# A hybrid decoder step on one core: a normalisation moved to ScalarE for a third token group, GpSimd and SyncE loads held by a VectorE instruction, and block-product operands paired otherwise

## The chip, the core and the metric

The kernel runs on one core of a Trainium2 chip. The core has five engines, each with its own instruction queue that it works in order: TensorE (PE in the profile; matrix products and transposes), VectorE (DVE), ScalarE (ACT), GpSimd (POOL) and SyncE (SP). Engines wait for each other through semaphores. All but PE and VectorE also start DMA transfers here, and a transfer's start stands in the queue of the engine that starts it. The metric is device time in microseconds (us); lower is better.

## The reference

One layer: a modulated RMSNorm, one input projection, two groups of heads (a gated linear recurrence, RG-LRU, and gated linear attention, GLA), one output projection, a gate, the residual and a last RMSNorm. There are 2048 prompt tokens of 1024 features and 8 single tokens of decoding ("samples") with their own state.

```python
hn = _rmsnorm(x, g_norm) * (1.0 + scale[:, None]) + shift[:, None]
z = hn @ w_in
xa, za, q, k, v, glr, zg = jnp.split(z, SPLITS, axis=-1)
...
a = jnp.exp(log_a)
u = mult * (gx * xc).astype(f32)
_, h = lax.associative_scan(_lin_comb, (a, u), axis=1)
y_lru = h.astype(x.dtype) * jax.nn.silu(za)
...
o, S_new = _gla_chunked(qh, kh, vh, log_alpha, S0.astype(f32))
o = o * lax.rsqrt(jnp.mean(o * o, axis=-1, keepdims=True) + EPS) * g_gla_norm.astype(f32)
y_gla = o.reshape(Bn, T, D_GLA).astype(x.dtype) * jax.nn.silu(zg)
mix = jnp.concatenate([y_lru, y_gla], axis=-1) @ w_out
x = x + gate[:, None] * mix
```

The columns of `w_in` are called XA, ZA, Q, K, V, GLR and ZG in the kernel. `xc` is a convolution over four tokens of `xa`, `h` the recurrence; v has 4 heads of 256 columns, and GLR's 16 columns drive the decay of the attention.

## The kernel before

**Numbers.** Every large product is made of three: a float32 operand is split into a rounded half (`hh`, "hi") and the remainder (`hl`, "lo"), and hi·hi, hi·lo and lo·hi are summed in PSUM, PE's accumulator memory. `hh` and `hl` hold the normalised input of 1024 tokens, features on the partitions, as (128, 8, 1024+64). So a line of products in the profile has two sisters (L661, L662, L663; L346, L347, L348).

**Halves.** The prompt is worked in two halves of 1024 tokens. In each half the four attention heads come in the order `HEADS` = 3, 0, 1, 2, and between them the tiles of the recurrence (128 channels each). Work that an engine is to do "somewhat later" is put on a list (`after(units, fn)`) and taken from it when `tick` has counted that many units; a second list, `drips`, is emptied one entry at a time between products.

**Between the halves** `hh` and `hl` are filled anew: `modulate(xt, g, kts)` takes one of four groups of 256 tokens (g = 0 to 3), two feature tiles (k2, k2+1) at a time. PE transposes four 128×128 blocks into a PSUM buffer of the tag "tp", of which there are two (L197). ScalarE scales and shifts the first feature tile out of it (L199); the second goes to ScalarE (L201) for g < 2, else to VectorE (L203). GpSimd rounds into `hh` (L204), and VectorE subtracts for `hl` (L205). Ahead of a group, VectorE multiplies its rows with reciprocal roots (L181). At the same time the first half's last recurrence tile runs (L1304 to L1338), and ZG of the first head (`gates_ahead`; L661–663, L1115, L1116, the store L1633 from ScalarE's queue).

**Block products.** For the second half, ZG of three heads and XA and ZA of two recurrence tiles are made by a scheme that needs seven block products in place of eight (`seven`, `product`, PE line L1545; five such sevens, so 35 operands of weights). The sums of blocks that it needs are made in `sums` (L1479 to L1488). The sums overwrite a quarter of the normalised input (`a21()`, the first four feature tiles of tokens 512 to 1023, 1 MB in `hh` and 1 MB in `hl`); a copy is kept in DRAM (`a21d`). An operand of weights is 512 KB, loaded by SP (L1527), and two operands share one buffer of the tag "w", of which there are three (`operand`): 1 and 2, 3 and 4, and so on; the 35th has a buffer to itself. A buffer is free when both its operands are used.

**A head of the second half** (`gla_head(1, h, ahead)`): `value_weights` has SP load the split weights of V in two parts of 1 MB (L293, tag "w"). For the first head, GpSimd then reads `a21` back (L1164–1166). `values` makes eight tiles of 128 tokens (L346–348; n = 272 columns for the first head, which has GLR with it, 256 for the others); each is copied out by ScalarE (L944) and VectorE (L945), and for the first head the 16 GLR columns are transposed and copied by VectorE (L876–878). Tiles 4 to 7 are the tokens that `a21` belongs to. At tile 2, `raw_values` starts two loads of the unsplit weights on GpSimd (L333, 512 KB each, tag "wr", of which there are two), which `sample_values` uses for the 8 samples (PE L900, VectorE L904) after the eight tiles; the first 32 matmuls of L900 use the first load, the other 32 the second. Then the decay, Q and K follow in segments, the chunks of the attention (L1029 and others), and the next recurrence tile, whose XA weights are loaded by `ahead` (SP, L293).

GpSimd's queue in these heads also has `zs<-zgd` (L1196, gates read back), and the preparation of output weights: `r` loads from `w_out` (L817), VectorE's products and sums (L838), and stores `wd<-r`, `wd<-t` (L852).

**Final products.** Before the end of the second half, `early` holds the first steps of the final products: for two pairs, `first` adds two blocks of `mixd` that SP loaded to `wr` (L1949), subtracts a third (L1950) and splits (L1680, L1683).

**Order.** A scheduler decides each engine's order from the traced program; the order of tracing counts, and so do waits. `behind(q)` (L683) adds an edge to the scheduler's order alone: what is traced inside is not issued ahead of the last instruction traced on q. It makes no semaphore wait.

Of the kernel before, what the change touches and what calls it, by code (L numbers as in the profile page):

```python
# [8 lines left out]
F32 = mybir.dt.float32  # L9
# [3 lines left out]
OP = mybir.AluOpType  # L13
# [41 lines left out]
def hybrid_kernel(ctx, tc, i, o):  # L55
# [131 lines left out]
    def modulate(xt, g, kts):  # L187

        c = slice(g * 256, (g + 1) * 256)
        for k2 in range(kts[0], kts[1], 2):  # L190
            pt = tps().rearrange("p (k t) -> p k t", k=2)
            cg = slice(g % 2 * 256, g % 2 * 256 + 256)
            f = (fs4[(1, 2, 0)[k2 // 4 if g < 2 else 2]][:, k2 % 4:k2 % 4 + 2, cg] if g < 2 or k2 >= 4
                 else ra[k2 // 2][:, :, cg])
            for kt in range(2):
                for j in range(2):
                    PE.transpose(pt[:, kt, j * P:(j + 1) * P],  # L197
                                 xt[j][:, (k2 + kt) * P:(k2 + kt + 1) * P], ident)
            S.activation(f[:, 0], pt[:, 0], AF.Identity, scale=Gm[:, k2, 8:9], bias=Sh[:, k2, 8:9])  # L199
            if g < 2:  # L200
                S.activation(f[:, 1], pt[:, 1], AF.Identity, scale=Gm[:, k2 + 1, 8:9], bias=Sh[:, k2 + 1, 8:9])  # L201
            else:
                V.tensor_scalar(f[:, 1], pt[:, 1], Gm[:, k2 + 1, 8:9], Sh[:, k2 + 1, 8:9], op0=OP.mult, op1=OP.add)  # L203
            G.tensor_scalar(hh[:, k2:k2 + 2, c], f, 1.0, 0.0, op0=OP.mult, op1=OP.add)  # L204
            V.tensor_tensor(hl[:, k2:k2 + 2, c], f, hh[:, k2:k2 + 2, c].bitcast(F32), op=OP.subtract)  # L205
# [118 lines left out]
    def value_weights(h):  # L324
        n = DV + (RANK if h == HEADS[0] else 0)
        return [weights(V0 + h * DV, n, k0, 4) for k0 in (0, 4)]
# [356 lines left out]
        return tc.issue_after(next(x for x in reversed(list(nc.cur_bb.bb.instructions)) if x.engine == q.engine))  # L683


    pend = []
    clock = [0, 0]

# [229 lines left out]
            e[2]()  # L918
        return [[gp.tile([P, 4, DV], F32R, tag=tag, name=tag, bufs=2) for _ in range(2)] for tag in ("vh", "vl")]

    def values(half, h, w):
        first = h == HEADS[0]
        n = DV + (RANK if first else 0)
        vh, vl = new_values()
        turns = []
        for tt in range(8):
            if tt == 2 and half == 1:
                raw = raw_values(h, n)
            if tt == 4:
                while drips:  # L930
                    drip()
            if half == 0 or tt < 6:
                ps = acc()
                value_mm(ps[:, :n], slice(tt * P, (tt + 1) * P), w, n, (0, KT))
            elif tt == 6:
                both = [acc(), acc()]
                for k in (0, 4):
                    for m in range(2):
                        value_mm(both[m][:, :n], slice((6 + m) * P, (7 + m) * P), w, n, (k, k + 4))
                ps = both[0]  # L940
            else:
                ps = both[1]
            hi, lo = vh[tt // 4][:, tt % 4], vl[tt // 4][:, tt % 4]
            S.copy(hi, ps[:, :DV])  # L944
            V.tensor_tensor(lo, ps[:, :DV], hi.bitcast(F32), op=OP.subtract)  # L945
            if len(turns) == 3 or tt == 7 and turns:
                turns.pop(0)()
            if first:
                turns.append(low_rank(ps[:, DV:n], slice(0, P), tt * P))
            tick(0.5)  # L950
        if half == 1:
            turns.append(sample_values(h, raw, n))
        for f in turns:
            after(1, f, True)
        return vh, vl
# [201 lines left out]
    def gla_head(half, h, wv=None, ahead=None):  # L1157
        ns = len(SEGS[half])
        if wv:
            wk, wq = wkq0  # L1160
            v, prep0, rest = first_head()
        else:
            w = value_weights(h)
            if half and h == HEADS[0]:  # L1164
                for u, x in enumerate(a21()):
                    G.dma_start(x.bitcast(F32), a21d[u])
            v = values(half, h, w)
            wk = weights(K0 + h * DK, DK)
            wq = weights(Q0 + h * DK, DK)
        prep, zs, os_, state = {}, {}, [None], []  # L1170

        def chunks(s, c):

            nch = min(SEGS[half][s][1], TH - SEGS[half][s][0]) // P
            if c == 0:
                prep[s, "run"] = gla_start(half, h, s, prep[s])
                after(PACE[half][0], lambda: chunks(s, 1), True, True)
                return
            if c == nch and half:
                gate_load(s)  # L1180
            gla_chunk(half, h, s, c - 1, prep[s], prep[s, "run"], v)
            if c < nch:
                after(PACE[half][1], lambda: chunks(s, c + 1), True, True)
                return
            gla_norm(nch, prep[s, "run"])
            after(PACE[half][2] if half else 1 if s + 1 < ns else 2, lambda: finish(s), True)
            if s + 1 < ns:
                after(0, lambda: chunks(s + 1, 0), True, True)
            elif half == 1:
                G.dma_start(o[4][0, 0, h], St[h])  # L1190

        def gate_load(s):
            c0, n = SEGS[half][s]
            for dt in range(2):
                z = new_zs()
                G.dma_start(z[:, :n], zgd[2 * h + dt][:, c0:c0 + n])  # L1196
                zs[s, dt] = z[:, :n]

        def finish(s):
            if (s, 1) not in zs or (s == 2 and os_[0] is None):  # L1200
                after(0.5, lambda: finish(s), True)
                return
            gla_out(half, h, s, prep[s, "run"][1], os_[0] if s == 2 else None, [zs[s, 0], zs[s, 1]])

        def sample(smp, b0):
            sample_state(h, smp, b0, state, lambda: os_.__setitem__(0, state[1]))

        pk = None
        if not wv:
            if h == HEADS[0]:  # L1210

                pk = project(wk, *SEGS[half][0])
            dec = gla_decay(half, h, 0)
        for s in range(ns):
            if wv and s == 0:
                prep[s] = prep0
                pk = project(wk, 512, 512)
                rest()
            else:
                prep[s] = gla_qk(half, h, s, wq, wk, dec, pk)  # L1220
                pk = None
                if s == 0 and ahead:
                    with behind(V):
                        ahead()
            if s + 1 < ns:
                dec = gla_decay(half, h, s + 1)
            if s == 0:
                after(2 if h == HEADS[0] else 1, lambda: chunks(0, 0), True, True)
            tick()
        if half == 1:  # L1230
            after(1, lambda: sample(prep[2][3], 0), True)
            after(3, lambda: sample(prep[2][3], 4), True)
        if wv:
            modulate_samples(st, xsr)
            hn_sample()
            with tc.issue_after(last[V.engine]), tc.issue_after(last[S.engine]):
                constants()
            open_lp()
        if half == 1:
            return  # L1240
        wz = [weights(ZG + (2 * h + dt) * P, P) for dt in range(2)]
        for s in range(ns):
            for dt in range(2):
                zs[s, dt] = gate_silu(wz[dt], s, 2 * h + dt)
                tick()
# [266 lines left out]
        for n, u in ((0, 0), (1, 0), (0, 1), (1, 1), (2, 0), (2, 1), (3, 0), (3, 1), (4, 0), (4, 1)):  # L1512
            drips.append(lambda n=n, u=u: step(n, u))

    operands, zq, zturn = [], [], [0]

    def operand(src, shifted):

        if operands:
            c = 568 if shifted else 576  # L1520
            w = operands.pop()
        else:
            c = 56 if shifted else 0
            w = wp.tile([P, 2, 1088], F32R, tag="w", name="w", bufs=3)
            operands.append(w)
        w = w[:, :, c:c + 512]
        SP.dma_start(w.bitcast(F32), src)  # L1527
        return w.rearrange("p u (k n) -> p u k n", k=4)
# [413 lines left out]
    for x in pairs[:2]:  # L1942
        x.new(A11)
        r = wp.tile([P, 1088], F32, tag="wr", name="wr")[:, :D].rearrange("p (q k t) -> p q k t", q=2, k=4)
        SP.dma_start(r, mixd[2 * x.p + 1, :, CTS[0]:CTS[0] + 8].rearrange("p (q k) t -> p q k t", q=2))
        SP.dma_start(x.lo(A11), x.rows(0, 0))

        def first(x=x, r=r):
            V.tensor_tensor(r[:, 0], r[:, 0], r[:, 1], op=OP.add)  # L1949
            V.tensor_tensor(r[:, 0], r[:, 0], x.lo(A11), op=OP.subtract)  # L1950
            x.s[S2] = r[:, 0]
            x.split(A11)

        early += [first, lambda x=x: x.split(S2)]
# [288 lines left out]
```

## Time and profile before

| | us |
|---|---|
| three runs | 1466.02, 1466.95, 1469.85 |
| median | 1466.95 |
| the profiled execution, its own time | 1465.58 |
| its span, first to last instruction | 1463.8 |
| PE busy in the span | 1427.3 (98%) |
| VectorE busy | 1053.7 (72%) |
| ScalarE busy | 688.0 (47%) |
| GpSimd busy | 221.3 (15%) |

The mean granted clock of TensorE over the span is 0.994 of full speed. Rows of the timeline read: start, duration, engine, line, operation, output<-inputs, shapes, how many instructions (x); in brackets the idle time of the engine before it and what ended it (`<-DVE ra L203`: the wait ended when VectorE's line 203 had written `ra`). Rows of stretches read: from:to and length, then busy us and number of instructions for PE, PE's weight loads, VectorE, ScalarE and GpSimd, then the granted clock, the DMA engines' busy share and GB/s. In the list of waits the three figures are the total, the number and the longest.

### The profile page before, as it was taken

Reading aid. Unit: us, or ns where it says so; the run is one execution under the profiler, and the core shown is the slowest. Engines: PE = TensorE matmul, PEld = TensorE weight load, DVE = VectorE, ACT = ScalarE, POOL = GpSimd, SP = SyncE. Lnnn points to the kernel's source line nnn. Section 1 sums busy time; section 2 is a strip of 40 time slices with the busy share of each in tenths; the row PEclk is TensorE's granted clock in tenths of the full one; section 3 lists DMA queues with packets and bytes.
Section 4 is the critical chain, followed back from the end, with each engine's and each line's share of the span. In section 5 each row is a group of like instructions: output and inputs, shape, how many; then the busy total and the mean of one; then the engine's idle time right before and its main releaser. Section 6 shows DMA issues by size and latency. Waiting matters only on the chain. (4 is left out here: it accounts for less than half of the span.)

```text
span 1463.8 us, 23573 instructions
## 1 busy us (share of the span) xinstructions
PE 1427.3 (98%) x8741; PEld 1254.7 (86%) x8741; DVE 1053.7 (72%) x2481; ACT 688.0 (47%) x1247; POOL 221.3 (15%) x366
## 2 busy tenths in 40 slices
PE   7999999999999998999899999999999999999998
PEld 6888989899898987878799999999899887778886
DVE  5757657776666778845358688586788986688886
ACT  4644544652445457524354454535558622144342
POOL 0200111112121122100212332323200000000000
PEclk9999999999999999999999999999999999999999
DMA  9755876765666455567736665666453767694453
GB/s 332 259 184 173 268 250 212 253 218 180 201 200 218 131 185 204 191 221 242 278 122 205 221 207 168 209 209 227 163 196 110 273 209 271 238 360 124 141 174 115
DMA packets 161240, 305.33 MB, mean 209 GB/s; under 512 B 12962, under 2 KB 91458, under 8 KB 158685
## 3 DMA queue, kind: packets, MB, share of 16 engines
q1 hardware_dynamic: 104917, 214.24, 42.8%
q0 software_dynamic: 23296, 72.54, 14.6%
q10 hardware_dynamic: 32912, 17.04, 3.8%
q8 instruction: 69, 1.13, 0.3%
q14 instruction: 46, 0.38, 0.1%
HBM read 188.51 MB, written 115.33 MB: 208 GB/s over the span
## 5 line engine op out<-in xcount | busy, mean ns | idle before, releaser
L661 PE MATMUL acc<-hh,w 128*128 128x512 f32 (+3 forms) x1112 | 387.1, 348 | 0.3 <-ACT tg L1304 0.2
L662 PE MATMUL acc<-hl,w 128*128 128x512 f32 (+3 forms) x1112 | 376.3, 338 | 0.0
L663 PE MATMUL acc<-hh,w 128*128 128x512 f32 (+3 forms) x1112 | 375.8, 338 | 0.0
L661 PEld LDWEIGHTS acc<-hh,w 128*128 128x128 f32 x1112 | 210.3, 189 | 17.8 <-ACT tx L1304 0.5
L662 PEld LDWEIGHTS acc<-hl,w 128*128 128x128 f32 x1112 | 210.3, 189 | 17.5 <-issue 1.2
L663 PEld LDWEIGHTS acc<-hh,w 128*128 128x128 f32 x1112 | 210.0, 189 | 16.4
L1830 PE MATMUL acc<-w,a 128*128 128x512 f32 (+1 forms) x792 | 184.9, 387 | 0.0
L1830 PEld LDWEIGHTS acc<-w,a 128*128 128x128 f32 x792 | 146.8, 188 | 33.2 <-issue 3.4
L346 PE MATMUL acc<-w,hh 128*128 128x256 f32 (+1 forms) x508 | 145.3, 286 | 3.7 <-DMA w<-parts 3.7
L348 PE MATMUL acc<-w,hl 128*128 128x256 f32 (+1 forms) x508 | 143.7, 283 | 0.2 <-DVE hl L228 0.2
L347 PE MATMUL acc<-w,hh 128*128 128x256 f32 (+1 forms) x508 | 143.7, 283 | 0.0
L1830 PE MATMUL tp<-w,a 128*128 128x512 f32 x564 | 136.3, 391 | 0.3 <-DVE w L1683 0.3
L1830 PEld LDWEIGHTS tp<-w,a 128*128 128x128 f32 x564 | 105.2, 188 | 27.4 <-issue 5.1
L346 PEld LDWEIGHTS acc<-w,hh 128*128 128x128 f32 x508 | 96.5, 190 | 5.2 <-DMA w<-parts 3.9
L348 PEld LDWEIGHTS acc<-w,hl 128*128 128x128 f32 x508 | 96.8, 191 | 0.4 <-DVE hl L228 0.4
L347 PEld LDWEIGHTS acc<-w,hh 128*128 128x128 f32 x508 | 96.2, 189 | 0.2
L1115 ACT ACTIVATE zs<-acc 128x512 f32<-128x512 f32 (+3 forms) x70 | 34.3, 491 | 110.2 <-PE acc L663 107.7
L1264 DVE SCALAR_TENSOR_TENSOR cv<-xa,vecT,cv 128x512 f32<-128x512 f32 (+2 forms) x120 | 76.2, 638 | 6.8 <-ACT cv L1262 6.3
L1680 ACT CAST a<-s 128x512 fp32r<-128x512 f32 x61 | 36.5, 620 | 94.5 <-issue 34.0
L1116 DVE SCALAR_TENSOR_TENSOR zs<-zs,acc 128x512 f32<-128x512 f32 (+3 forms) x70 | 38.5, 550 | 48.6 <-ACT zs L1115 48.6
L944 ACT CAST vh<-acc 128x256 fp32r<-128x256 f32 x56 | 20.6, 370 | 97.6 <-PE acc L348 84.1
L945 DVE TENSOR_TENSOR vl<-acc,vh 128x256 fp32r<-128x256 f32 x56 | 23.3, 421 | 55.7 <-ACT vh L944 55.5
(404 smaller groups left out, 2749.4 us busy)
## 6 DMA issues: line engine op xcount, KB each, us to landing
parts<-w SPq DMA_DIRECT2D x37, 1024.0 KB
w<-parts SPq DMA_DIRECT2D x28, 1024.0 KB
wr<-in_w_in_dram SPq DMA_DIRECT2D x38, 512.0 KB
a<-mixd SPq DMA_DIRECT2D x63, 256.0 KB
w<-wd SPq DMA_DIRECT2D x12, 1024.0 KB
w<-twd SPq DMA_DIRECT2D x20, 512.0 KB
mixd<-zs ACTq DMA_DIRECT2D x34, 256.0 KB
wada<-in_w_ada_dram SPq DMA_DIRECT2D x16, 512.0 KB
```

The source lines that it names most:

```text
L346: PE.matmul(ps, hh[:, kt, c], hi[:, kt % 4], start=kt == 0, stop=False)
L347: PE.matmul(ps, hh[:, kt, c], lo[:, kt % 4], start=False, stop=False)
L348: PE.matmul(ps, hl[:, kt, c], hi[:, kt % 4], start=False, stop=kt == KT - 1)
L661: PE.matmul(ps[:, :n], hi[:, kt], a, start=kt == 0, stop=False)
L662: PE.matmul(ps[:, :n], hi[:, kt], b, start=False, stop=False)
L663: PE.matmul(ps[:, :n], lo[:, kt], a, start=False, stop=kt == KT - 1)
L945: V.tensor_tensor(lo, ps[:, :DV], hi.bitcast(F32), op=OP.subtract)
L1115: S.activation(z, ps, AF.Tanh, scale=0.5)
L1116: V.scalar_tensor_tensor(z, z, 1.0, ps, op0=OP.add, op1=OP.mult)
L1264: V.scalar_tensor_tensor(cv[:, cq], xa[:, cq.start + k:cq.stop + k], cw[k], cv[:, cq], op0=OP.mult, op1=OP.add)
L1680: S.copy(t[:, 0, k], (low(t) if src is None else src)[:, k])
L1830: PE.matmul(ps, t[:, u, k], w[:, v, k, c], start=(q < 3 or ps is own) and (k, u, v) == (0, 0, 0), stop=(k, u) == (3, 1), skip_group_check= ...
```

## The change

It has six parts.

1. `modulate`: the second feature tile goes to ScalarE for g < 3 instead of g < 2. For g = 2 four instructions of L203 become instructions of L201.
2. A new helper, `held(q)`: every SP or GpSimd instruction traced inside waits, by a semaphore, for the last instruction traced on engine q.
3. `values`: the two reads of `a21` (first head of the second half) are started at tile 1 instead of before tile 0, and held by VectorE. `raw_values` is started at tile 3 instead of tile 2, held by VectorE, in all four heads of the second half.
4. `gla_head`: the next recurrence tile's XA weights (`ahead`) are held by VectorE instead of ordered by `behind`.
5. `operand`: the first operand has a buffer to itself, and the pairs are 2 and 3, 4 and 5, up to 34 and 35.
6. `first`: its first sum (L1949) is under `behind(V)`.

In the built program, PE's own instructions keep their order everywhere except in `values` for the first head of the second half: after the change, the products of tiles 0 to 3 run in order, then three transposes of GLR, then four pairs of products with `hh` (L346, L347) ahead of the first with `hl` (L348), and a few more such exchanges in the tiles behind; before, the transposes stand between the tiles and the exchanges in the first tile. VectorE's L1949 stands some 75 us later in its queue. GpSimd's queue has, for the second head of the second half: a store `wd<-r`, the first raw load, two stores `wd<-t`, two `r` loads, the second raw load; for the third: two `r` loads and then both raw loads; for the fourth: the first raw load, two `r` loads, the second raw load. In the first head, four `zgd` stores and the loads of `g` and `bt` stand ahead of the reads of `a21`.

```diff
--- before.py
+++ after.py
@@ -197,7 +197,7 @@
                     PE.transpose(pt[:, kt, j * P:(j + 1) * P],
                                  xt[j][:, (k2 + kt) * P:(k2 + kt + 1) * P], ident)
             S.activation(f[:, 0], pt[:, 0], AF.Identity, scale=Gm[:, k2, 8:9], bias=Sh[:, k2, 8:9])
-            if g < 2:
+            if g < 3:
                 S.activation(f[:, 1], pt[:, 1], AF.Identity, scale=Gm[:, k2 + 1, 8:9], bias=Sh[:, k2 + 1, 8:9])
             else:
                 V.tensor_scalar(f[:, 1], pt[:, 1], Gm[:, k2 + 1, 8:9], Sh[:, k2 + 1, 8:9], op0=OP.mult, op1=OP.add)
@@ -683,6 +683,18 @@
         return tc.issue_after(next(x for x in reversed(list(nc.cur_bb.bb.instructions)) if x.engine == q.engine))
 
 
+    @contextmanager
+    def held(q):
+
+        traced = nc.cur_bb.bb.instructions
+        mark = next(x for x in reversed(list(traced)) if x.engine == q.engine)
+        before = {id(x) for x in traced}
+        yield
+        for x in list(traced):
+            if id(x) not in before and x.engine in (SP.engine, G.engine):
+                tc.add_manual_dep(x, mark.name, mybir.DependencyInfo(
+                    mybir.DependencyClass.Sync, mybir.DependencyReason.DATA), reason="held")
+
     pend = []
     clock = [0, 0]
 
@@ -918,14 +930,18 @@
             e[2]()
         return [[gp.tile([P, 4, DV], F32R, tag=tag, name=tag, bufs=2) for _ in range(2)] for tag in ("vh", "vl")]
 
-    def values(half, h, w):
+    def values(half, h, w, back=None):
         first = h == HEADS[0]
         n = DV + (RANK if first else 0)
         vh, vl = new_values()
         turns = []
         for tt in range(8):
-            if tt == 2 and half == 1:
-                raw = raw_values(h, n)
+            if tt == 1 and back:
+                with held(V):
+                    back()
+            if tt == 3 and half == 1:
+                with held(V):
+                    raw = raw_values(h, n)
             if tt == 4:
                 while drips:
                     drip()
@@ -1160,11 +1176,10 @@
             wk, wq = wkq0
             v, prep0, rest = first_head()
         else:
-            w = value_weights(h)
+            w, back = value_weights(h), None
             if half and h == HEADS[0]:
-                for u, x in enumerate(a21()):
-                    G.dma_start(x.bitcast(F32), a21d[u])
-            v = values(half, h, w)
+                back = a21_back
+            v = values(half, h, w, back)
             wk = weights(K0 + h * DK, DK)
             wq = weights(Q0 + h * DK, DK)
         prep, zs, os_, state = {}, {}, [None], []
@@ -1220,7 +1235,7 @@
                 prep[s] = gla_qk(half, h, s, wq, wk, dec, pk)
                 pk = None
                 if s == 0 and ahead:
-                    with behind(V):
+                    with held(V):
                         ahead()
             if s + 1 < ns:
                 dec = gla_decay(half, h, s + 1)
@@ -1512,7 +1527,11 @@
         for n, u in ((0, 0), (1, 0), (0, 1), (1, 1), (2, 0), (2, 1), (3, 0), (3, 1), (4, 0), (4, 1)):
             drips.append(lambda n=n, u=u: step(n, u))
 
-    operands, zq, zturn = [], [], [0]
+    def a21_back():
+        for u, x in enumerate(a21()):
+            G.dma_start(x.bitcast(F32), a21d[u])
+
+    operands, lone, zq, zturn = [], [True], [], [0]
 
     def operand(src, shifted):
 
@@ -1522,7 +1541,9 @@
         else:
             c = 56 if shifted else 0
             w = wp.tile([P, 2, 1088], F32R, tag="w", name="w", bufs=3)
-            operands.append(w)
+            if not lone:
+                operands.append(w)
+            lone.clear()
         w = w[:, :, c:c + 512]
         SP.dma_start(w.bitcast(F32), src)
         return w.rearrange("p u (k n) -> p u k n", k=4)
@@ -1946,7 +1967,8 @@
         SP.dma_start(x.lo(A11), x.rows(0, 0))
 
         def first(x=x, r=r):
-            V.tensor_tensor(r[:, 0], r[:, 0], r[:, 1], op=OP.add)
+            with behind(V):
+                V.tensor_tensor(r[:, 0], r[:, 0], r[:, 1], op=OP.add)
             V.tensor_tensor(r[:, 0], r[:, 0], x.lo(A11), op=OP.subtract)
             x.s[S2] = r[:, 0]
             x.split(A11)
```

## The prediction, made before the changed kernel ran

> **What bounds the kernel now.** I read the busy shares first, then what TensorE (PE) waited for, then stretches of the span around the longest of those waits.
>
> ```profile
> PE 1427.3 (98%) x8741; PEld 1254.7 (86%) x8741; DVE 1053.7 (72%) x2481; ACT 688.0 (47%) x1247; POOL 221.3 (15%) x366
> PE tp L197 <- DVE ra L203: 4.4, 1, 4.4
> PE tp L1029 <- DVE xb L1014: 4.2, 3, 2.6
> PE acc L346 <- DMA w<-parts: 3.7, 1, 3.7
> PE acc L1545 <- DVE ra L1483: 1.0, 1, 1.0
> 579.00:583.40 4.40, 0.05 (x1) 0.05 (x1) 4.32 (x12) 0.00 (x0) 0.00 (x0) 0.88 0.00 0
> 583.40:590.20 6.80, 6.80 (x37) 6.80 (x37) 4.72 (x9) 1.51 (x3) 2.44 (x4) 0.58 0.12 41
> 718.85:722.30 3.45, 3.45 (x15) 3.45 (x16) 0.00 (x0) 0.34 (x1) 2.09 (x3) 0.51 1.01 401
> ```
>
> PE is busy 1427.3 of 1463.8 us, so only 36.5 us of the span are not its work. No part of this change removes a matrix product, so the change can win only what PE waits, plus what follows a wait. The waits' columns are total, number of times, longest: three single waits (4.4, 2.6 and 3.7 us) stand out, each at a place that the diff touches. The stretches show the second price: behind the first wait the granted clock (the figure before the last two of a row) is 0.58 for 6.8 us, behind the third 0.51 for 3.45 us. At about half speed that is another 3.4 and 1.7 us of work not done.
>
> **The change part by part.** All times are positions in the old span.
>
> (A) Third group of tokens, g<3. Four second halves (k2 = 0, 2, 4, 6) move from VectorE (DVE) L203 to ScalarE (ACT) L201.
>
> ```profile
> 583.35 1.11 PE L197 MATMUL tp<-ident,xst 128*128 128x128 f32 x4 [4.36 <-DVE ra L203]
> 582.10 0.74 DVE L181 TENSOR_SCALAR xt<-xt,rs 128x1024 f32<-128x1024 f32 x1
> 582.76 0.99 DVE L203 TENSOR_SCALAR ra<-tp,Gm,Sh 128x256 f32<-128x256 f32 x2
> 583.66 0.41 DVE L1116 SCALAR_TENSOR_TENSOR zs<-zs,acc 128x256 f32<-128x256 f32 x1
> 584.11 0.34 ACTq L1633 DMA_DIRECT2D zgd<-zs  x1
> L201 ACT ACTIVATE fs<-tp,Sh,Gm x8: 555/568/607, 563.0 to 573.0; 128x256 f32<-128x256 f32 x8
> 589.78 0.27 PE L197 MATMUL tp<-ident,xst 128*128 128x128 f32 x1
> 591.01 0.55 DVE L203 TENSOR_SCALAR ra<-tp,Gm,Sh 128x256 f32<-128x256 f32 x1 [0.45 <-ACT ra L199]
> 624.59 0.50 PE L1545 MATMUL acc<-ra,w 128*128 128x512 f32 x1 [1.04 <-DVE ra L1483]
> ```
>
> PE cannot reuse a transpose buffer until both its readers are done; L203 stood in VectorE's queue behind the reciprocal roots and two L181, ScalarE was idle. After the change the two readers end on ScalarE by about 579, so the 4.36 us go, and with them 3.4 us of slow clock: at most 7.8. But ScalarE meets its next queue entry, L1633, which waits for L1116. VectorE now has one L205 there instead of the two L203 (0.99), so L1116 ends about 583.8 instead of 584.07, L1633 about 584.1, and L199 with L201 for the third transposes (0.56 and 0.57 us) about 585.1. PE, 7.8 us early, reaches the next group's transposes (row 589.78) near 582.0 and stands until 585.1: a new wait of 3.1, and a gain of 589.78 − 585.1 = 4.7. Behind it, group four keeps its L203 on VectorE, whose serial chain (L203, the copy on GpSimd, L205) starts at 591.01 and moves only 3.4 to 3.9 us forward. From there VectorE works without a gap up to the wait at 624.59, so its lead is the smaller. I take −3.7; bounds −7.8 (the new wait does not come) and −2.0 (it drops the clock, which costs 1.7).
>
> (B) First head of the second half: value weights and a21. L1164–1166 (two 1 MB reads into hh and hl) and the raw value weights leave the start, and the lone operand shifts the pairs so that the buffer for the second half of the weights comes free one product sooner.
>
> ```profile
> 709.94 3.25 SPq L293 DMA_DIRECT2D w<-parts  x2
> 712.47 0.28 PE L346 MATMUL acc<-w,hh 128*128 128x272 f32 x1
> 718.85 0.59 PE L346 MATMUL acc<-w,hh 128*128 128x272 f32 x1 [3.69 <-DMA w<-parts]
> 703.64 0.77 POOL L333 DMA_DIRECT2D wr<-in_w_in_dram  x1 [0.49 <-issue]
> 707.68 0.75 POOL L1166 DMA_DIRECT2D hh<-a21d  x1 [0.26 <-issue]
> DMA to landing us min/median/max: 9.4/11.6/13.7
> 717.08 1.28 DVE L1338 SCALAR_TENSOR_TENSOR zs<-tg,zs 128x512 f32<-128x512 f32 x2
> ```
>
> The load is issued at 709.94 and PE resumes at 718.85: 8.9 us, beside the GpSimd loads. One product is 12 matmuls at 0.227 us, 2.7 us; it now starts about 707.2, is wanted at about 715.0, and both a21 reads and the raw loads are no longer beside it. 7.8 us for a load that took 8.9 with 3 MB more beside it: in time. That removes 3.69 and 1.7 of slow clock: −5.4 (bound −3.5 if a wait of 1.9 stays).
>
> New wait: the a21 reads are held by the last VectorE instruction of tile 0. VectorE ends its two L1338 at 718.4 and the tile's four small ones near 719.3; in GpSimd's queue the reads stand behind four zgd stores and two loads, and behind them in turn stand the r loads and raw_values. PE runs tiles 0 to 3 from 712.47 in 4×24×0.127 = 12.2 us and wants hh at 724.7, hl at 725.8 (the transposes and eight products come between). About 2.9 MB at the 401 GB/s of the stretch above is 7 us from 719.5: hl at 726.5 to 727. By the landings of the old reads (last row but one: 9.4 and 13.7 us from issue) it is 728.7 and 733.5. I take +1.2, since the load that shared those old transfers is gone; bounds 0 and +7.7, or 9.4 with 1.7 of slow clock.
>
> (C) `first` (L1949) behind VectorE.
>
> ```profile
> 1024.16 0.69 DVE L1949 TENSOR_TENSOR wr<-wr 128x512 f32<-128x512 f32 x1 [2.07 <-DMA wr<-mixd]
> 1027.77 0.94 PE L1029 MATMUL tp<-xb,e 128*128 128x128 f32 x6 [2.63 <-DVE xb L1014]
> 1095.00:1112.00 17.00, 16.38 (x104) 15.40 (x103) 17.00 (x42) 14.22 (x29) 0.00 (x0) 1.00 0.40 121
> ```
>
> VectorE stood 2.07 us for a load, and L1008 and L1014, which PE needed, stood behind it. After the change L1949 is issued where the rest of `first` is, some 75 us later, and the load has long landed: −2.6 (it alone waited 2.07 and twice 0.69 were worked before L1014, so nothing of the 2.63 need stay; bound −2.0). The price: VectorE is full there (17.00 of 17.00), two of 0.69 us; PE is not short of other work for most of it: +0.5, bounds 0 and 1.4.
>
> (D) Raw value weights (four heads), now at tile 3 and held by VectorE's last instruction of tile 2. Before, each head's two loads were issued a head ahead.
>
> ```profile
> 835.05 0.76 POOL L333 DMA_DIRECT2D wr<-in_w_in_dram  x1 [2.31 <-PE acc L900]
> 834.07 1.08 PE L900 MATMUL acc<-wr,fs 128*8 128x64 f32 x64
> 924.25 1.08 PE L900 MATMUL acc<-wr,fs 128*8 128x64 f32 x64
> 1014.47 1.08 PE L900 MATMUL acc<-wr,fs 128*8 128x64 f32 x64
> 825.39 0.42 DVE L945 TENSOR_TENSOR vl<-acc,vh 128x256 fp32r<-128x256 f32 x1
> 1006.75 0.42 DVE L945 TENSOR_TENSOR vl<-acc,vh 128x256 fp32r<-128x256 f32 x1
> 830.76 1.44 POOL L817 DMA_DIRECT2D r<-in_w_out_dram  x2
> 1011.16 1.45 POOL L817 DMA_DIRECT2D r<-in_w_out_dram  x2 [1.38 <-DMA wd<-r]
> wr<-in_w_in_dram POOLq DMA_DIRECT2D x2, 512.0 KB, 5.4
> wr<-in_w_in_dram POOLq DMA_DIRECT2D x2, 512.0 KB, 7.4
> DMA to landing us min/median/max: 4.9/6.5/8.1
> DMA to landing us min/median/max: 3.1/4.7/9.1
> ```
>
> The row at 835.05 is the load for the head after: it had 89 us. Now tile 2's L945 (825.39, 1006.75) must be over, and L900 wants the second half of the weights half its 1.08 us after its start: 834.6, 924.8, 1015.0. The built order decides more than the mark. GpSimd issues the first load at once, but the second after the wd stores and the r loads, which wait for a store to land: about 830.7 for the second head, 918.3 for the third, 1012.6 (1011.16 + 1.45) for the fourth. Of the last four rows, two give what such loads took from 743.9 (5.4) and from 835.05 beside SP's loads (7.4), the third is for all of L333's in the second half, and the fourth for the r loads of half the size. By 5.4 the landings are 836.1, 923.7 and 1018.0: waits of 1.5, 0 and 3.1, so +4.6. I take 5.4 because one load of 0.5 MB now flies where two did. By 8.1: 4.2, 1.6 and 5.7, so 11.5, with two stretches of slow clock 14.9. By 3.1, the quickest row: 0, 0 and 0.7. The first head has nothing to lose: wanted at 742.8, issued near 726.
>
> [...]
>
> (E) At nothing.
>
> ```profile
> 831.35 28.20 SPq L293 DMA_DIRECT2D w<-parts  x3
> ```
>
> Of these three loads the next tile's XA weights, held instead of ordered, go out near 845 instead of 834. The head's remaining segments on PE hide that; without them it would cost the load's landing, 7 us by the row of 7.4. The other operands keep a lead of about four products, 4×12×0.227 = 10.9 us, over loads half the size of those in (B).
>
> Sum: −3.7 − 5.4 + 1.2 − 2.6 + 0.5 + 4.6 = −5.4. The profiled execution took 1465.58 us (1463.80 of span and 1.78 around it), so 1460.2; it lies 1.37 under the median of 1466.95, by which the change gives 1461.5. A difference under 0.3%, 4.4 us, cannot be told from none, so the edges are 1462.6 and 1471.3.
>
> **The rivals**, on the median.
>
> 1. The raw loads are not late: they land in about 3.1 us, as the quickest L817 did, D is +0.7, and the time 1457.6. For it: GpSimd's loads no longer go out in pairs. Against: SP issues 1 MB loads in the same microseconds (row 7.4). [...]
> 2. At g = 2 the change doesn't do what it says: VectorE, not the transpose buffer, is the bound from 579 to 625. It keeps its L181 and L205, and the lead in (A) ends up in longer waits at 614.8 and 624.6. A is 0: 1465.2, no difference. For it: VectorE's unbroken queue up to 624.59. Against: the 3.4 us of slow clock in 583.40:590.20 are PE's alone, and VectorE still leads by 3.4.
> 3. Slower: the second raw load of the second and fourth head takes the place of the waits removed. Its place is L900, its price 14.9 instead of 4.6, its time 1471.8. It decides from a landing of about 8 us, when the waits pass the 3.69 us that dropped the clock here, where 2.63 (1027.77) is followed by none of it. Speaking for it: the maximum of 8.1 and the row of 7.4. Against: the 5.4, and the third head, whose 6.5 us from 918.3 would do even so.
> 4. The read-back of a21 is late: it lands 13.7 us after issue, tile 4 stands 7.7 us and the clock drops, 9.4 instead of 1.2: 1469.7, no difference. For it: 2 MB behind one mark; against: the stretch it flies in has lost 2 MB of others.
>
> [...]
>
> **How the numbers follow.** Forecast 0.45, rival 1 0.22, rival 2 0.16, rival 3 0.11, rival 4 0.06. Two thirds of the forecast's own spread (1458.5 to 1464.5, A and B within half their bounds) lie under 1462.6, as does rival 1; with a quarter of rival 2 that is 0.56 faster. Slower is rival 3 and the upper edge of rival 4: 0.13. The rest, 0.31, is within 0.3%. The range takes rivals 1, 2 and 4 whole, with A's better bound below 1457.6 (−3.5 or so): 1454 to 1470.
>
> **What would show it.** A: PE's wait on L203 at 583 gone; a wait on ACT of about 3.1 at the fourth group; granted clock 1.00 behind it. If longer waits at L1545 appear, it is rival 2. B: no wait on w at 718; instead one at tile 4 on DMA hh or hl, of 1 us; 8 would be rival 4. C: no L1949 before L1029's wait. D: new waits of PE L900 on DMA wr, 1.5 and 3.1; none makes it rival 1, over 3.7 with slow clock rival 3. What would make the prediction wrong outright is a scheduler's order on the chip in which another engine's queue, SP's loads above all, is shifted by the held instructions so that PE waits for a load that no row above names.

## The result, and the profile after

The changed kernel takes 1477.55 us (median of four runs, 1476.86 to 1478.24) against 1466.77 for the kernel before (four runs). The ratio is 1.0070, 95% interval 1.0052 to 1.0087: slower by 10.8 us, where 5.4 less was forecast. In what follows 0.1% is 1.47 us.

The page and the list of waits of the changed kernel (total, number, longest):

```profile
PE 1435.1 (97%) x8741; PEld 1262.3 (86%) x8741; DVE 1052.0 (71%) x2477; ACT 688.7 (47%) x1251; POOL 220.5 (15%) x366
PE acc L912 <- DMA wr<-in_w_in_dram: 9.7, 3, 4.8
PE tp L197 <- ACT fs L201: 3.4, 1, 3.4
PE acc L346 <- DMA hh<-a21d: 2.4, 1, 2.4
PE acc L1566 <- ACT acc L1580: 1.8, 1, 1.8
PE acc L348 <- DMA hl<-a21d: 0.9, 1, 0.9
```

The three long waits of before are gone; these stand in their place. (L912 was L900, L1566 was L1545.) The span is 1475.4, 11.6 more than before, and it divides unevenly: TensorE's idle time rose by 3.8 us (40.3 for 36.5), its busy time by 7.8, with the same 8741 products. The same work taking longer points to the granted clock. The stretches behind the new waits:

```profile
586.20:593.00 6.80, 6.80 (x45) 6.80 (x46) 4.12 (x8) 3.09 (x7) 2.50 (x4) 0.75 0.11 39
614.80:618.20 3.40, 3.40 (x10) 2.66 (x9) 3.40 (x4) 0.13 (x1) 0.00 (x0) 0.51 0.89 301
728.83:734.30 5.47, 5.47 (x24) 5.47 (x25) 0.00 (x0) 0.08 (x1) 1.80 (x3) 0.50 0.79 286
838.24:845.00 6.76, 6.76 (x54) 6.55 (x55) 2.86 (x10) 4.60 (x7) 2.04 (x4) 0.61 0.13 49
1026.04:1032.80 6.76, 6.76 (x54) 6.55 (x55) 2.86 (x10) 4.60 (x7) 2.03 (x4) 0.61 0.51 181
```

Length times (1 − clock) is 1.7, 1.7, 2.7, 2.6 and 2.6: 11.3 us of work, against 4.5 for the two such stretches of before (6.8 at 0.58 and 3.45 at 0.51). The difference, 6.8, is most of the 7.8 us that the products take longer.

Where the time went is seen from the same instructions in both timelines. The first fence has two of before that the prediction did not need, the second those of after:

```profile
742.78 1.13 PE L900 MATMUL acc<-wr,fs 128*8 128x68 f32 x64
1454.04 3.03 PE L1830 MATMUL acc<-w,a 128*128 128x256 f32 x24
```

```profile
586.20 0.33 PE L197 MATMUL tp<-ident,xst 128*128 128x128 f32 x1 [3.45 <-ACT fs L201]
711.41 0.28 PE L346 MATMUL acc<-w,hh 128*128 128x272 f32 x1
742.66 1.14 PE L912 MATMUL acc<-wr,fs 128*8 128x68 f32 x64
833.17 0.63 PE L912 MATMUL acc<-wr,fs 128*8 128x64 f32 x32
838.24 1.04 PE L912 MATMUL acc<-wr,fs 128*8 128x64 f32 x32 [4.44 <-DMA wr<-in_w_in_dram]
929.23 0.63 PE L912 MATMUL acc<-wr,fs 128*8 128x64 f32 x32
1020.64 0.63 PE L912 MATMUL acc<-wr,fs 128*8 128x64 f32 x32
1026.04 1.04 PE L912 MATMUL acc<-wr,fs 128*8 128x64 f32 x32 [4.77 <-DMA wr<-in_w_in_dram]
1465.66 3.03 PE L1851 MATMUL acc<-w,a 128*128 128x256 f32 x24
```

| place | before | after | shift |
|---|---|---|---|
| first transposes of the fourth token group | 589.78 | 586.20 | −3.6 |
| first value product | 712.47 | 711.41 | −1.1 |
| samples' products, first head | 742.78 | 742.66 | −0.1 |
| second head | 834.07 | 833.17 | −0.9 |
| third head | 924.25 | 929.23 | +5.0 |
| fourth head | 1014.47 | 1020.64 | +6.2 |
| last products | 1454.04 | 1465.66 | +11.6 |

Up to the second head the gains of A and B had been given back almost wholly. The third head's products then lie 5.9 us further back than the second's, and the last products 5.4 us further than the fourth head's: between them stand the waits of 4.44 and 4.77, each with 2.6 us of slow clock behind it, less what other places gained. The rows behind the first of these waits, from GpSimd's queue at the second head, and the landings of the two raw loads issued at 826.19 and 830.48:

```profile
826.19 0.76 POOL L333 DMA_DIRECT2D wr<-in_w_in_dram  x1 [0.18 <-issue]
826.94 1.08 POOL L864 DMA_DIRECT2D wd<-t  x2
829.05 1.44 POOL L829 DMA_DIRECT2D r<-in_w_out_dram  x2 [1.03 <-DMA wd<-r]
830.48 0.77 POOL L333 DMA_DIRECT2D wr<-in_w_in_dram  x1
DMA to landing us min/median/max: 5.3/5.3/5.3
DMA to landing us min/median/max: 7.7/7.7/7.7
```

The second load was issued at 830.48 (forecast 830.7) and wanted at 833.8; it took 7.7 us where 5.4 was assumed. At the fourth head it took 8.1.

### The profile page after: what moved, and what is told of

The parts are those of the page before. It is cut to its first block, busy times and chain, and to the rows that moved or that the text cites. A ratio compares the mean times of both kernels' runs of the same rounds, so it can differ in the third digit from the quotient of the medians.

```text
span 1475.4 us, 23576 instructions
## 1 busy us (share of the span) xinstructions
PE 1435.1 (97%) x8741; PEld 1262.3 (86%) x8741; DVE 1052.0 (71%) x2477; ACT 688.7 (47%) x1251; POOL 220.5 (15%) x366
## 5 line engine op out<-in xcount | busy, mean ns | idle before, releaser
L346 PE MATMUL acc<-w,hh 128*128 128x256 f32 (+1 forms) x508 | 145.4, 286 | 2.5 <-DMA hh<-a21d 2.4
L348 PE MATMUL acc<-w,hl 128*128 128x256 f32 (+1 forms) x508 | 144.1, 285 | 0.9 <-DMA hl<-a21d 0.9
L347 PE MATMUL acc<-w,hh 128*128 128x256 f32 (+1 forms) x508 | 144.1, 284 | 0.0
L346 PEld LDWEIGHTS acc<-w,hh 128*128 128x128 f32 x508 | 97.0, 191 | 3.9 <-issue 2.7
L348 PEld LDWEIGHTS acc<-w,hl 128*128 128x128 f32 x508 | 97.1, 192 | 1.3 <-DMA hl<-a21d 1.3
L347 PEld LDWEIGHTS acc<-w,hh 128*128 128x128 f32 x508 | 97.0, 191 | 0.2
L1701 ACT CAST a<-s 128x512 fp32r<-128x512 f32 x61 | 36.5, 619 | 96.1 <-issue 36.6
L1132 DVE SCALAR_TENSOR_TENSOR zs<-zs,acc 128x512 f32<-128x512 f32 (+3 forms) x70 | 38.5, 550 | 46.8 <-ACT zs L1131 46.7
```

The lines of the kernel that those rows point to most:

```text
L346: PE.matmul(ps, hh[:, kt, c], hi[:, kt % 4], start=kt == 0, stop=False)
L347: PE.matmul(ps, hh[:, kt, c], lo[:, kt % 4], start=False, stop=False)
L348: PE.matmul(ps, hl[:, kt, c], hi[:, kt % 4], start=False, stop=kt == KT - 1)
L1132: V.scalar_tensor_tensor(z, z, 1.0, ps, op0=OP.add, op1=OP.mult)
L1701: S.copy(t[:, 0, k], (low(t) if src is None else src)[:, k])
```

## The experiments

Each kernel was timed against the kernel before on the same chip; that kernel's median was 1468.5, 1467.5, 1468.3 and 1468.2 us in the four sets of experiments. Kernels of different sets are compared by their ratios to it, and percentage points below are differences of these ratios.

| kernel | median us | ratio to before | 95% interval |
|---|---|---|---|
| changed | 1477.55 | 1.0070 | 1.0052 to 1.0087 |
| raw_free | 1463.70 | 0.9965 | 0.9953 to 0.9978 |
| a21_early | 1469.83 | 1.0011 | 0.9998 to 1.0025 |
| g2_dve | 1481.75 | 1.0086 | 1.0063 to 1.0109 |
| raw_on_sp | 1466.42 | 0.9982 | 0.9972 to 0.9993 |
| combo | 1456.23 | 0.9916 | 0.9891 to 0.9940 |
| combo_store_sp | 1454.61 | 0.9900 | 0.9880 to 0.9921 |
| held_alone | 1477.81 | 1.0060 | 1.0039 to 1.0081 |
| first_alone | 1463.76 | 0.9975 | 0.9962 to 0.9989 |
| combo_g2 | 1460.05 | 0.9952 | 0.9938 to 0.9966 |
| lone_alone | 1464.45 | 0.9966 | 0.9947 to 0.9984 |
| combo_lone_off | 1463.08 | 0.9967 | 0.9956 to 0.9979 |
| wx_plain | 1475.67 | 1.0064 | 1.0042 to 1.0086 |
| raw_tile0 | 1463.09 | 0.9963 | 0.9949 to 0.9977 |

### The raw value weights (D)

raw_free: three heads' raw loads as before the change.

```diff
-            if tt == 3 and half == 1:
+            if tt == 2 and half == 1 and not first:
+                raw = raw_values(h, n)
+            if tt == 3 and half == 1 and first:
                 with held(V):
                     raw = raw_values(h, n)
```

> The changed kernel (1477.5) with the raw value weights of the second to fourth head started at tile 2 and not held, as before the change; the first head's stay held. Theory: what the change lost is the second raw load standing late in GpSimd's queue (waits of 4.44, 0.53 and 4.77 us at the samples' products, and slow clock behind two of them): these waits are gone and the time falls by 10 to 13, to about 1465. Rival: the waits only show first what another stage would have shown next (VectorE, other loads), and less than half comes back: over 1471.

1.05 percentage points less than the changed kernel, 15 us, a little over what the theory gave; no wait at the samples' products is left in its trace, and nothing took its place. The rival falls.

held_alone: the kernel before, with the helper `held` and only this part of the change.

```diff
-            if tt == 2 and half == 1:
-                raw = raw_values(h, n)
+            if tt == 3 and half == 1:
+                with held(V):
+                    raw = raw_values(h, n)
```

> The kernel before with one part alone: raw value weights at tile 3 and held by VectorE, in all four heads. Theory: the waits at the samples' products come with this part alone, 10 to 15 us; in the first head the later raw loads leave room for the value weights, and the old wait for w (3.69) shrinks to 1 or 2: in sum 8 to 13 more than before. Rival: the waits need the other parts (held XA weights, earlier tiles) and are under 2 us each: less than 3 more than before.

0.60% more, 8.8 us. In its list of waits, two at the samples' products, of 5.36 and 6.79:

```profile
PE acc L912 <- DMA wr<-in_w_in_dram: 12.1, 2, 6.8
```

The wait for w shrank from 3.69 to 2.82. So the part does this alone, as the theory said.

raw_on_sp: what makes the second load late, the hold or the place in GpSimd's queue?

```diff
 def raw_values(h, n):
...
-            G.dma_start(r[-1], i["w_in"][...
+            SP.dma_start(r[-1], i["w_in"][...
```

> The changed kernel with all raw value weights started from SP's queue in place of GpSimd's, still held by the same VectorE instruction at tile 3. Theory: not the hold but the place in GpSimd's queue (behind output-weight loads that wait for stores) makes the second load late: both loads start within 1 us of the hold, land before they are wanted, and the time is about 1465. Rival: the hold on VectorE, or the bandwidth beside the K and Q weights, makes it late: waits of 3 us and more stay at the samples' products, time over 1474.

0.88 points less than the changed kernel, 13 us. With the same hold, both loads go out right behind the mark (827.62), and the 64 products run through:

```profile
827.62 0.42 DVE L961 TENSOR_TENSOR vl<-acc,vh 128x256 fp32r<-128x256 f32 x1
828.07 0.98 SPq L333 DMA_DIRECT2D wr<-in_w_in_dram  x2
833.58 0.53 SPq L293 DMA_DIRECT2D w<-parts  x1
836.30 1.08 PE L912 MATMUL acc<-wr,fs 128*8 128x64 f32 x64
```

But the K weights, 1 MB, now start at 833.58 instead of 830.55. That left open whether the second load had been late for its start or for the K weights beside it. raw_tile0 leaves SP's queue as it is and has the raw loads of the last three heads wait for an earlier VectorE instruction (the last one ahead of tile 0 instead of tile 3), by which both stand ahead of the `r` loads in GpSimd's queue at the second and fourth head:

```diff
-            if tt == 3 and half == 1:
+            if tt == (3 if first else 0) and half == 1:
                 with held(V):
```

> The changed kernel with the raw value weights of the second to fourth head held by the VectorE instruction ahead of tile 0 in place of tile 3's; the orders of TensorE, VectorE, ScalarE and SP are unchanged. For the second and fourth head both raw loads now stand ahead of the r loads in GpSimd's queue, for the third the second one still stands behind them; SP's K weights start as in the changed kernel. Theory: the start decides: no wait over 1 at the second and fourth head's samples' products, and 9 to 14 less than the changed kernel, 1464 to 1469. Rival: the K weights beside them decide, as they started later too where the loads were put on SP: waits of 2 or more stay at both heads, less than 6 below the changed kernel.

```profile
824.11 1.53 POOL L333 DMA_DIRECT2D wr<-in_w_in_dram  x2
833.26 1.44 POOL L829 DMA_DIRECT2D r<-in_w_out_dram  x2 [4.92 <-DMA wd<-r]
830.73 0.53 SPq L293 DMA_DIRECT2D w<-parts  x1
DMA to landing us min/median/max: 6.9/7.3/7.8
833.45 1.08 PE L912 MATMUL acc<-wr,fs 128*8 128x64 f32 x64
```

1.07 points less than the changed kernel, 16 us, a little more than expected. The K weights start as in the changed kernel, the two loads take 6.9 and 7.8 us, about what the late one did (7.7), and no wait is left at the samples' products: the start decides. The `r` loads now start 4.2 us later, but the raw loads were no quicker for it. The hold costs nothing here, where both loads start over 8 us ahead of the products.

### The a21 reads (B)

```diff
             if half and h == HEADS[0]:
-                back = a21_back
+                a21_back()
```

> The changed kernel with the two a21 reads started before the values and not held; all else as changed. Theory: their hold costs the waits of 2.41 and 0.92 us at tile 4 and some 2.7 of slow clock behind them, and the value weights no longer need the room, as their load now starts 3.8 us earlier: no wait of TensorE from 711 to 742, time lower by about 6, 1471.5. Rival: the reads beside the weights bring the old wait for w back (3.7 and slow clock): 1476 to 1478, no gain.

0.59 points less than the changed kernel, 8.7 us: more than the 6 expected. GpSimd's and SP's rows show why the old wait does not come back. The second half of the value weights starts at 705.56, 4.4 us earlier than before the change, and the reads at 706.32 and 708.77, 13 and 12 us earlier than with the hold; both have landed when they are wanted:

```profile
705.07 0.55 POOL L1627 DMA_DIRECT2D zgd<-zq  x1 [22.16 <-DVE zq L1132]
706.32 0.77 POOL L1532 DMA_DIRECT2D hh<-a21d  x1 [0.71 <-issue]
708.77 0.76 POOL L1532 DMA_DIRECT2D hl<-a21d  x1
705.56 5.97 SPq L293 DMA_DIRECT2D w<-parts  x2
```

TensorE does not wait once over 0.5 us from 614 to 778. The remaining 9.9 us at the samples' products stay. Part of the surplus over 6 can be chance: in the changed kernel the wait of 1.82 at the first block product was followed by a clock of 0.51 for 3.4 us, 1.7 us of lost work, and in wx_plain a wait of 2.03 at the same place by 1.00; a21_early waits 2.35 there.

combo: both together.

> The changed kernel with both of these: raw value weights of the second to fourth head as before the change, and the a21 reads started before the values and not held. Theory: the two losses lie apart in time and add, and what is left of the change (g<3, the lone operand, first behind VectorE, XA weights held) is a gain: no wait of TensorE over 1.1 from 711 to 1030, and 11 to 14 us less than the kernel before. Rival: with the a21 reads early and the raw loads free, loads pile up again at the second half's first head and the gain over the kernel before stays at the 5 that the free raw loads gave alone.

0.84% less than before, 12.3 us; the two losses add, and no wait over 1.1 is left from 711 to 1030.

### The pairing of operands

lone_alone is the kernel before with this part alone; combo_lone_off is the combination without it.

```diff
-    operands, zq, zturn = [], [], [0]
+    operands, lone, zq, zturn = [], [True], [], [0]
...
-            operands.append(w)
+            if not lone:
+                operands.append(w)
+            lone.clear()
```

> The kernel before with one part alone: the first operand in a buffer of its own. Theory: the value weights' second half starts 2.7 to 3.8 earlier, the wait of 3.69 shrinks to under 1 and the slow clock behind it goes: 3 to 5.4 less than before. Rival: the raw weights and a21 reads that fly at the same time set its landing, and the wait stays over 2.5: within 1.5 of before.

0.34% less, 5.0 us; medians 3.9. The load starts at 705.92 instead of 709.94, and the wait shrinks to 1.96, not to under 1, with a clock of 0.64 in the 3.4 us behind it. Its profiled execution (1468.96) is the slowest of ten and also shows waits of 3.18 and 3.21 at 839 and 1030, so its other rows are not typical of the median.

> The combination with operands paired as before (1 and 2, 3 and 4). Theory: the value weights start at the old time with the a21 reads beside them and without the raw loads: a wait for w of 1 to 2.5, with or without slow clock, 1.5 to 4 more than the combination. Rival: the raw loads alone were in the way, the pairing does nothing: within 0.7 of the combination.

0.51 points more than the combination, 7.5 us, nearly twice the upper end of what was expected: the wait for w is 2.87, and the clock drops to 0.50 behind it. The pairing is worth its place even with the raw loads out of the way. Neither of the two removes the wait alone: 1.96 was left with the pairing, 2.87 here and 2.82 in held_alone with the raw loads later; with both it is gone.

### The activations on ScalarE (A)

```diff
-            if g < 3:
+            if g < 2:
```

> The changed kernel with g<2 as before. Theory: the move to ScalarE, which removed 4.36 us of waiting, gave most of it back (3.45 on ScalarE, 1.82 at the first block products, both with slow clock), and was worth about 1.1: 1478.6. Rival 1: it was worth the forecast 3.7 and later stages lost it for other reasons: 1481.2. Rival 2: it does harm, and the time falls below 1477.

0.16 points more than the changed kernel, 2.3 us, inside the intervals' width: between theory and rival 1. Its trace differs at a later place too (the wait for the a21 reads is 4.53), so the two cannot be told apart here. In the combination it is more:

> The combination (raw value weights of three heads free, a21 reads early and free) with g<2 as before. Theory: the move to ScalarE keeps a worth of 1 to 3 where nothing behind it waits for loads: 1.5 to 3 more than the combination. Rival: VectorE sets the pace from 579 to 625 and the move is worth nothing: within 0.7 of the combination.

0.36 points, 5.3 us, above the range. In the changed kernel the first block product waits 1.82 behind the earlier work and the clock drops to 0.51 for 3.4 us; in the combination it waits 1.73, and behind 1.66 at the same place in combo_g2 the clock stays at 1.00. So, by an estimate from these traces, 1.7 us of this part's worth can hang on such an accident.

combo_store_sp asks where the new wait of 3.45 comes from.

```diff
-                after(0.5, lambda ...: S.dma_start(zgd[...], z))
+                after(0.5, lambda ...: SP.dma_start(zgd[...], z))
```

> As the run above, and the gate stores between the halves (zgd<-zs) started from SP's queue in place of ScalarE's. Theory: the new wait of 3.45 at the fourth token group comes from such a store, which stands in ScalarE's queue ahead of the third group's activations and waits for VectorE: the wait shrinks to about 1 or goes, as does the slow clock behind it, and the time falls by another 2 to 4. Rival: the fourth group's rows (L181 on VectorE) are as late: the wait stays above 2.5 and the time is that of the run above within 1.

ScalarE's rows in the changed kernel: the store waits for VectorE's L1132, the third group's activations stand behind it, and TensorE at 586.20 behind them.

```profile
584.66 0.34 ACTq L1654 DMA_DIRECT2D zgd<-zs  x1
585.12 0.56 ACT L199 ACTIVATE fs<-tp,Sh,Gm 128x256 f32<-128x256 f32 x1 [5.85 <-DVE zs L1132]
585.59 0.56 ACT L201 ACTIVATE fs<-tp,Sh,Gm 128x256 f32<-128x256 f32 x1
```

And without the store in that queue:

```profile
584.62 0.30 PE L197 MATMUL tp<-ident,xst 128*128 128x128 f32 x1 [1.22 <-DVE xst L181]
584.62:591.40 6.78, 6.42 (x52) 6.03 (x53) 5.51 (x11) 2.36 (x5) 0.92 (x2) 1.00 0.13 43
```

The wait is 1.22 and ends on VectorE's L181, the clock stays at 1.00: the mechanism is shown. The time is 1.6 us under the combination, less than expected and not beyond the intervals. Where the rest of the gain goes is not shown: the waits at the block products are 1.22 and 0.80, against 1.73 and 0.97 in the combination. At 0.9900 of before this was the fastest kernel measured.

### The two small parts

first_alone is the kernel before with L1949 behind VectorE:

> The kernel before with one part alone: the first sum of the final products behind VectorE. Theory: the wait of 2.63 at L1029 goes and little is given back: 1.5 to 2.6 less than before. Rival: VectorE is full where the sums land and gives all of it back at the last recurrence tiles: within 0.7 of before.

0.25% less, 3.7 us (interval 1.6 to 5.6). In the trace the 2.63 at L1029 is gone, but waits of 1.05 and 1.39 stand at the last recurrence tiles (1104.92 and 1123.86), where the kernel before had none over 0.5. By the trace most of it is given back, by the medians it is not; the profiled execution is one of the two slowest of ten, so the trace does not settle it.

wx_plain is the changed kernel with the next tile's XA weights ordered instead of held:

> The changed kernel with the next recurrence tile's XA weights ordered behind VectorE in place of held, as before. Theory: no matter, within 1 of the changed kernel, 10 to 12 more than before. Rival 1: the hold is what keeps these loads clear of the raw value weights, and without it the waits at the samples' products grow: 2 or more above the changed kernel. Rival 2: the hold delays SP's later loads: 2 or more below.

0.06 points below the changed kernel: no difference, as the theory said.

## Why the prediction was wrong

D is the step that turned the sign: 4.6 us were taken for it, and the waits at L912 (9.7) and the slow clock behind two of them (5.2) came to 14.9. The place was right (L900, second and fourth head), and so were the issue times, 830.48 for the forecast 830.7. What failed is "I take 5.4 because one load of 0.5 MB now flies where two did": the landings were 7.7 and 8.1. The nearest old load said so. The 7.4 given for 835.05 is the median of two, and the load issued at 835.05 itself, 3 us ahead of the other and beside SP's weights, took:

```profile
DMA to landing us min/median/max: 8.1/8.1/8.1
```

That is `before`, in us. The other, from 838.11, took 6.7. The row 4.9/6.5/8.1 is not of all L333 loads of the second half either: it has five of eight, and the others took 4.4, 7.6 and 4.0. (The wait of 3.1 at the fourth head is 3.0 by its own figures, which changes nothing.)

Why the loads took 7.7 and 8.1 stays open. At the second head the two r loads (0.5 MB) start 1.4 us ahead of the raw load, the K weights (1 MB) with it, and three gate reads behind it; but raw_tile0's loads, which start ahead of the K weights and of the r loads, took 6.9 and 7.8. Undoing the part gave 15 us, and starting the loads earlier 16. So what is shown is rival 3's mechanism, from the landing of about 8 us that it named. That its price, 14.9, was met is partly chance: it was made of 11.5 of waits and 3.4 of slow clock, where 9.7 and 5.2 came.

D was not all. Without it the forecast's sum is −10.0, and raw_free, which undoes it for three heads, measured 5 us less than before. The other misses, in A, B, C and the clock, follow.

The slow clock was the second failure, and ran through A, B and D. The forecast let no drop follow the waits it took as likeliest, up to 3.1 us, because 2.63 had left none; that 3.1 would leave none too was its author's estimate, which no trace here shows: 3.18 (lone_alone) and 3.45 were followed by 0.50. Five drops came, 11.3 us of lost work, and that is more than all of the new waits at L912 (9.7). In rival 3 a drop was priced at 1.7; behind 4.44 and 4.77 it was 2.6. The slow clock of before was mis-sized too: 6.8 us at 0.58 is 2.9 us of lost work, not 3.4.

A: the mechanism was as forecast (new wait 3.1, measured 3.45, through the store in ScalarE's queue, shown by combo_store_sp). But it dropped the clock (0.75 over the 6.8 us behind it), the bound "−2.0", and a second wait of 1.82 at the block products was followed by 0.51 for 3.4 us: −1.1 at 711.41 for the forecast −3.7.

B: the old wait went, as forecast, through the earlier start. The reads were mis-sized: issued at 719.58 and 720.51, they landed after 6.7 and 8.3 us, and the two waits (2.41, 0.92) with their slow clock came to 6.0 where +1.2 was taken; the upper bound was 9.4. The size is not steady: in wx_plain's trace the wait for the same reads was 5.03 and ended at 728.09, in the changed kernel's at 726.41. With the operands paired anew the hold was not needed at all, as a21_early shows.

C and E: the wait at L1029 went as forecast. In the changed kernel's trace the later waits at the recurrence tiles come to 2.2 (0.88 and 1.35) instead of 0.5. Holding the XA weights cost nothing, as forecast.

Rivals 1, 2 and 4 did not come true: the loads were not quick, VectorE did not take back all of A up to 711, and the a21 reads were late by 3.3 and not by 7.7.

## What to carry to other kernels

A load that moves from a whole stage ahead to "just in time" is priced at the slowest landing seen in that stage (here 8.1, from the same place), not at a median, with everything named that starts in the same microseconds, and from its real place in its queue: here a start some 6 us earlier, from a place a few instructions ahead in GpSimd's queue, was worth 16 us. When a wait is traded for another, price the clock behind both: here slow clock (five stretches at 0.50 to 0.75, against two at 0.51 and 0.58 before) made 6.8 of the 11.6 us by which the span grew, and it shows as no wait. And try the parts of a change alone: here three of six (1, 5 and 6) gained, and the kernel that keeps them without the harmful holds beat the kernel before by 12 us while the whole lost 11.

## What the runs showed of the hardware

In these profiles no one length parts the waits of TensorE that a lower clock followed from those that none did. Eight profiles (before, changed, first_alone, lone_alone, combo_lone_off, combo_g2, wx_plain, raw_tile0), between 570 and 1200 us of each span, have 28 waits of 1.41 us and more:

| waits, us | how many | granted clock behind them |
|---|---|---|
| 1.41, 1.52, 1.66, 1.69 (lone_alone, combo_lone_off, combo_g2, raw_tile0) | 4 | 1.00 |
| 1.82 (changed) | 1 | 1.00 for 1.3 us, then 0.50 for 3.4 us |
| 1.96 (lone_alone) | 1 | 0.98 for 1 us, then 0.50 |
| 2.03 (wx_plain), 2.63 (before) | 2 | 1.00 |
| 2.41 (changed), 2.46 (raw_tile0), each with a second wait of 0.9 right behind it | 2 | 0.50 behind the second |
| 2.87 (combo_lone_off) | 1 | 0.86 for 1 us, then 0.50 |
| 3.18 to 5.88 | 17 | 16 with a stretch at 0.50; raw_tile0's 3.65: 0.75 over the 6.8 us behind it |

The same place shows both: the first block product waits 1.82 in the changed kernel, with the 0.50 behind it, and 2.03 in wx_plain with 1.00. Why the shorter one was followed by it and the longer one not, no run here shows.
